# Split right operands of a three-term FFN down product made during gate and up and kept in DRAM, with output pairs visited in turn

## The chip, the cores and the metric

The kernel runs on one NeuronCore of one Trainium2 chip. The metric is device time in microseconds of that core, from launch to end. Before the change the median of three runs is 2494.79 us (2493.0 to 2496.13).

## What is computed

A two-layer encoder trunk on 1024 positions of width 1024, all in f32. Each layer is a mixer, a cross-attention into 256 memory rows and a SwiGLU feed-forward block, each behind an RMSNorm and added onto x. The change touches the feed-forward block alone:

```python
def swiglu(h, w_gate, w_up, w_down):
    return (jax.nn.silu(h @ w_gate) * (h @ w_up)) @ w_down
# per layer: w_gate, w_up (1024, 2816), w_down (2816, 1024)
x = x + swiglu(rms_norm(x, g_ffn[layer]), w_gate[layer], w_up[layer], w_down[layer])
```

## The kernel before

**Three-term products.** An f32 operand is split into two f32r parts: a high part h, which is a cast on ScalarE, and a low part l = value - h, made on VectorE (`low`, L409). A product is three matmuls: wh*xh, wh*xl, wl*xh. Everything is kept transposed: a block row of x is 128 channels by 1024 positions.

**Seven products for eight.** The feed-forward products use a Strassen-Winograd scheme with two by two blocks (`seven`). A left operand (`Unit`) is n stacked pairs of weight rows by 256 columns; from it seven parts are made with four additions, each part 128 x n*128, on the engine named `adds`. A right operand (`Pair`) is two 128 x 1024 tiles, cut into four 128 x 512 blocks; from it seven operands of 512 columns are made with four GpSimd subtractions (L307), seven casts (L318) and seven low parts (L409). Each of the seven tasks of a unit runs 3n matmuls of 512 columns into one PSUM bank. Gate and up have n = 4 (width 1024 is four pairs): 84 matmuls a unit, 22 units a layer. Down has 11 pairs of FF rows and four column pairs of the output (mp = 0 to 3).

**After a task.** `collected` gathers gate's and up's results: ScalarE copies out of PSUM (L1756, L1762, L1764) and VectorE additions (L1754). For three of the four quarters a bank is added onto again one task after it was read. `gated` applies the norm and silu with a VectorE product (L1804), a ScalarE activation (L1805) and a GpSimd product (L1806). `upped` multiplies gate and up (L1813) and stores each finished 128 x 1024 tile to the DRAM tensor `pd` (L1818), 512 KB, two for each pair of units. `onto_x` adds down's banks onto x (L1785), eight additions a unit.

**Down.** The 11 pairs are taken in four groups, DOWN = (3, 3, 3, 2 pairs). In each group the pairs' tiles are loaded from `pd` (L1856), their operands are made (GpSimd, ScalarE, VectorE as above), and all four column pairs are run with them; the units' additions are on GpSimd too (L232).

**Memory and order.** Split operands live in one arena of f32r with 35 slots of 1024 columns (`R`; a pair of h and l of 512 columns takes one slot), f32 tiles in another with 16 (`F`). During gate and up 28 slots hold the four pairs of the normed x. `run` goes through the tasks, fetches weights ahead (at most `raws` heavy ones, `f_reserve` free) and makes operands ahead as long as they are within `la` columns of the running task and `reserve` columns stay free. A scheduler then orders each engine's queue; every DMA named here is issued by SyncE (SP), whose queue runs in order, and each of its DMAs waits for the one eight before it. Down_start raises `la` from 4096 to 16384 and loads x back from `xs`. `defer` runs a step some tasks later.

## Time and profile before

| | us |
|---|---|
| median of three runs | 2494.79 |
| profiled execution, its own time | 2492.48 |
| its span, first to last instruction | 2490.7 |
| TensorE busy | 2369.1 (95%) |
| VectorE busy | 1722.8 (69%) |
| ScalarE busy | 1026.5 (41%) |
| GpSimd busy | 853.0 (34%) |
| mean granted TensorE clock | 0.973 |

Busy time of TensorE is no measure of its pace, since matmuls are pipelined and their ends are modelled: a stretch in which it is 90% busy can hold 70% of the matmuls that fit. The number of matmuls in a stretch tells the pace. Gate and up of layer 0 run from about 700 to 1100 us and down from there to about 1370; gate and up of layer 1 from about 1785 to 2225 us and down from there to the end. The view by stage gives for each engine its busy time and, in brackets, its instructions, then the granted clock as a share, the mean busy share of the 16 DMA engines, and what they moved.

### The profile page before, as it was taken

The numbers are of one execution on the slowest core, as the hardware profiler recorded it, in microseconds if no ns is written. First come the engines' busy times: TensorE is split into PE (matmuls) and PEld (weight loads), VectorE is DVE, ScalarE is ACT, GpSimd is POOL, SyncE is SP. The second block draws the span as 40 slices with busy tenths as digits, with TensorE's granted clock in tenths as the row PEclk, the third lists the DMA queues.
The fourth block names the chain that finished last, engine by engine and source line by source line (L and its number), as shares of the span: only waits on it lengthen the run. The fifth ranks groups of instructions, "written<-read, shape, count | busy, mean of one in ns | idle before, by whom it ended". The sixth has DMA issues, their size and how long they took to land. (4 is left out here: it accounts for less than half of the span.)

```text
span 2490.7 us, 30370 instructions
## 1 busy us (share of the span) xinstructions
PE 2369.1 (95%) x11246; PEld 1978.2 (79%) x11246; DVE 1722.8 (69%) x2449; ACT 1026.5 (41%) x1886; POOL 853.0 (34%) x849
## 2 busy tenths in 40 slices
PE   7999999999899999998899999999799999989998
PEld 7998889888678888876677888888588887767776
DVE  5456367855686676689989643545876767589887
ACT  5355366645543333343335221244533333344332
POOL 6551233243531112136654300132721111146551
PEclk9999999999889999999999999999799999999999
DMA  7345345421231312243222121110321231243322
GB/s 233 124 144 172 94 119 141 132 76 35 102 102 51 102 60 85 93 139 110 93 89 81 60 59 35 59 43 18 118 85 68 93 102 51 74 164 102 102 87 74
DMA packets 175836, 234.83 MB, mean 94 GB/s; under 512 B 7200, under 2 KB 145528, under 8 KB 175688
## 3 DMA queue, kind: packets, MB, share of 16 engines
q1 hardware_dynamic: 171856, 220.10, 28.1%
q0 software_dynamic: 3648, 12.75, 1.4%
q8 instruction: 88, 1.44, 0.2%
q14 instruction: 60, 0.49, 0.1%
q10 hardware_dynamic: 184, 0.05, 0.0%
HBM read 176.11 MB, written 56.75 MB: 93 GB/s over the span
## 5 line engine op out<-in xcount | busy, mean ns | idle before, releaser
L397 PE MATMUL psum_t<-arena_r 128*128 128x512 f32 (+4 forms) x10304 | 2293.3, 381 | 99.1 <-DVE arena_r L409 43.4
L397 PEld LDWEIGHTS psum_t<-arena_r 128*128 128x128 f32 (+1 forms) x10304 | 1867.5, 191 | 473.9 <-DVE arena_r L409 67.1
L409 DVE TENSOR_TENSOR arena_r<-arena_f,arena_r 128x512 fp32r<-128x512 f32 (+4 forms) x839 | 739.0, 904 | 303.5 <-ACT arena_r L241 153.6
L241 ACT CAST arena_r<-arena_f 128x512 fp32r<-128x512 f32 (+2 forms) x532 | 288.8, 563 | 565.1 <-PE psum_t L397 402.3
L1806 POOL TENSOR_TENSOR arena_f<-arena_f 128x512 f32<-128x512 f32 x88 | 135.1, 1538 | 656.3 <-ACT arena_f L1805 656.1
L307 POOL TENSOR_TENSOR arena_f<-arena_f 128x512 f32<-128x512 f32 x120 | 184.1, 1550 | 120.4 <-DMA arena_f<-pd 58.2
L232 POOL TENSOR_TENSOR arena_f<-arena_f 128x384 f32<-128x384 f32 (+1 forms) x128 | 148.2, 1166 | 103.6 <-DVE arena_r L409 51.7
L1785 DVE TENSOR_TENSOR arena_f<-psum_t,arena_f 128x512 f32<-128x512 f32 x256 | 167.7, 680 | 15.7 <-PE psum_t L397 15.0
L318 ACT CAST arena_r<-arena_f 128x512 fp32r<-128x512 f32 x210 | 123.6, 617 | 124.9 <-POOL arena_f L307 62.4
L232 DVE TENSOR_TENSOR arena_f<-arena_f 128x512 f32<-128x512 f32 x176 | 136.0, 778 | 55.6 <-DMA arena_f<-w_up 34.2
L1754 DVE TENSOR_TENSOR arena_f<-psum_t,arena_f 128x512 f32<-128x512 f32 x176 | 119.9, 685 | 33.9 <-PE psum_t L397 28.3
L527 ACT CAST arena_r<-arena_f 128x1024 fp32r<-128x1024 f32 (+1 forms) x57 | 59.0, 1042 | 109.9 <-PE psum_t L397 99.5
L409 DVE TENSOR_TENSOR arena_r<-psum_t,arena_r 128x512 fp32r<-128x512 f32 (+3 forms) x124 | 84.7, 703 | 24.9 <-ACT arena_r L1596 8.7
L1805 ACT ACTIVATE arena_f<-arena_f 128x512 f32<-128x512 f32 x88 | 55.6, 632 | 99.7 <-DVE arena_f L1804 99.2
L633 POOL TENSOR_TENSOR arena_f<-arena_f 128x1024 f32<-128x1024 f32 x21 | 60.3, 2870 | 87.0 <-ACT arena_f L632 79.7
L1259 POOL TENSOR_SCALAR arena_f<-arena_f,small 128x640 f32<-128x640 f32 (+6 forms) x64 | 49.4, 780 | 108.6 <-DVE small L1258 104.6
L1813 DVE TENSOR_TENSOR arena_f<-arena_f 128x512 f32<-128x512 f32 x88 | 73.9, 841 | 3.3
L1804 DVE TENSOR_TENSOR arena_f<-arena_f 128x512 f32<-128x512 f32 x88 | 70.7, 804 | 0.8
L420 POOL TENSOR_TENSOR small<-small,mhalf 128x4 f32<-128x4 f32 (+1 forms) x64 | 64.3, 1005 | 5.2
L1705 POOL TENSOR_TENSOR arena_f<-arena_f 128x512 f32<-128x512 f32 x28 | 43.7, 1571 | 50.7 <-ACT arena_f L1704 50.2
L1948 POOL TENSOR_TENSOR arena_f<-arena_f 128x1024 f32<-128x1024 f32 x4 | 9.6, 2392 | 140.9 <-DVE arena_f L1900 136.1
L1254 ACT ACTIVATE arena_f<-psum_t,small 128x640 f32<-128x640 f32 (+6 forms) x64 | 47.5, 744 | 23.0 <-DVE small L1252 20.1
(177 smaller groups left out, 1390.9 us busy)
## 6 DMA issues: line engine op xcount, KB each, us to landing
arena_f<-w_gate SPq DMA_DIRECT2D x22, 1024.0 KB
arena_f<-w_up SPq DMA_DIRECT2D x22, 1024.0 KB
pd<-arena_f SPq DMA_DIRECT2D x44, 512.0 KB
arena_f<-pd SPq DMA_DIRECT2D x44, 512.0 KB
arena_f<-w_down SPq DMA_DIRECT2D x24, 768.0 KB
arena_f<-xs SPq DMA_DIRECT2D x32, 512.0 KB
arena_r<-qk SPq DMA_DIRECT2D x48, 256.0 KB
xs<-arena_f SPq DMA_DIRECT2D x24, 512.0 KB
```

The costliest lines, as they stand in the source:

```text
L232: getattr(T.nc, self.adds).tensor_tensor(out=out, in0=a, in1=b, op=what)
L241: T.nc.scalar.copy(out=hv, in_=src)
L307: getattr(T.nc, self.adds).tensor_tensor(out=out, in0=a, in1=b, op=ALU.subtract)
L318: T.nc.scalar.copy(out=h.ap, in_=src)
L397: self.nc.tensor.matmul(out=out, lhsT=lhsT, rhs=rhs, start=start, stop=stop, skip_group_check=again)
L409: getattr(self.nc, eng).tensor_tensor(out=out, in0=src, in1=high, op=ALU.subtract)
L420: self.nc.gpsimd.tensor_tensor(out=out, in0=in_, in1=self.mhalf[:, 0:in_.shape[-1]], op=ALU.pow)
L1754: nc.vector.tensor_tensor(out=o, in0=bank[q].ap, in1=o if other is None else other, op=ALU.add)
L1785: nc.vector.tensor_tensor(out=o, in0=bank[q].ap, in1=o, op=ALU.add)
L1804: nc.vector.tensor_tensor(out=q, in0=q, in1=r, op=ALU.mult)
L1806: nc.gpsimd.tensor_tensor(out=q, in0=q, in1=r, op=ALU.mult)
L1813: nc.vector.tensor_tensor(out=c[j].ap[:, o], in0=c[j].ap[:, o], in1=s.ap[:, o], op=ALU.mult)
```

## The change

The right operands of down are made once, while gate and up run, and kept split. When a pair of FF tiles is finished, `store` makes its seven operands in seven steps, one step a task: the same four GpSimd subtractions (L1860), a ScalarE cast (L1864) and a VectorE low part for each. Both parts of an operand lie in one slot of the arena and go as one 512 KB store to a DRAM tensor `pq` (L1868) one task later. In down an operand is a `Stored`: two loads of 256 KB straight into the f32r arena (L339), nothing else. The units' additions in down are on VectorE (the default of `adds`).

The order in down is no longer four groups by four column pairs but a list of 14 visits (mp, first pair, last pair): each visit runs one column pair over two to four FF pairs, and the window of pairs moves on. All 44 combinations are there once. The pairs from 9 on take slots from the other end of the arena, in layer 0 from there only. The last four visits close one column pair each; the squares for the next norm are taken there, while the norm's scaled chunks of the first two are made when the last two visits open (`chunk_done` is cut in `chunk_h` and `chunk_sq`). In gate and up `la` falls from 4096 to 2048 and `reserve` rises from 0 to 3072; in down `la` is 4096.

```diff
@@
-DOWN = ((0, 1, 2), (3, 4, 5), (6, 7, 8), (9, 10))
+VISITS = ((1, 0, 1), (2, 0, 1), (3, 0, 2), (0, 0, 3), (1, 2, 4), (2, 2, 5), (3, 3, 6), (0, 4, 7), (1, 5, 8), (2, 6, 8),
+          (3, 7, 10), (0, 8, 10), (1, 9, 10), (2, 9, 10))
@@ class Stored:
+    def make(self, T, must):
+        pair = T.room_for(512, self.home, must)
+        if pair is None:
+            return False
+        self.h, self.l = pair
+        for part, t in enumerate(pair):
+            T.nc.sync.dma_start(out=t.f, in_=self.src[part].bitcast(F32))
+        return True
@@ in upped:
-
-                    def keep():
-                        nc.sync.dma_start(out=self.pd[layer, (f + j) * P:(f + j + 1) * P, :], in_=c[j].ap)
-                        c[j].free()
-                    self.defer(keep)
+                if (j, half) == (0, 1):
+                    store(f // 2, c)
             return fn
 
+        def store(pr, c):
+
+            b11, b12 = c[0].ap[:, 0:512], c[0].ap[:, 512:1024]
+            b21, b22 = c[1].ap[:, 0:512], c[1].ap[:, 512:1024]
+            t1, t2 = self.F.get(512, "ba"), self.F.get(512, "ba")
+
+            def sub(out, a, b):
+                nc.gpsimd.tensor_tensor(out=out, in0=a, in1=b, op=ALU.subtract)
+
+            def part(i, src):
+                t = self.R.get(1024, "ab")
+                nc.scalar.copy(out=t.ap[:, 0:512], in_=src)
+                self.low(t.ap[:, 512:1024], src, t.f[:, 0:512])
+
+                def keep():
+                    nc.sync.dma_start(out=self.pq[layer, pr, i].rearrange("s p c -> p s c").bitcast(F32),
+                                      in_=t.f.rearrange("p (s c) -> p s c", s=2))
+                    t.free()
+                self.defer(keep)
...
+            for n in range(7):
+                self.defer(lambda n=n: step(n), n + 1)
+
         def start():
-            self.reserve, self.la, self.raws = 0, 4096, 2
+            self.reserve, self.la, self.raws = 3072, 2048, 2
@@ in down_start:
-            self.la, self.f_reserve = 16384, 0
+            self.reserve, self.la, self.f_reserve = 0, 4096, 0
...
+        for n, (mp, lo, hi) in enumerate(VISITS):
+            left = len(VISITS) - n
+            u = Unit(wd, lo * 256, hi - lo + 1, mp * 256, "b", "b" if finish and left <= 4 else "ba")
+            if left == 2 and finish:
+                self.add(open_now)
+            if left == 1:
+                self.add(down_end)
+            self.seven(u, ps[lo:hi + 1], self.onto_x(2 * mp, quarter_of(mp, left <= 2) if left <= 4 else None))
```

Two places in the built programs. **SyncE's queue from gate and up into down, layer 0.** Before: a few stores of `pd`, then loads of `pd` and blocks of `w_down` in turn, 512 KB and 768 KB each:

```order
L222 DMA arena_f<-w_gate 128x8x256
L1818 DMA pd<-arena_f 128x1024
L222 DMA arena_f<-w_up 128x8x256
L1818 DMA pd<-arena_f 128x1024
L222 DMA arena_f<-w_down 128x6x256
L1856 DMA arena_f<-pd 128x1024 x2
L222 DMA arena_f<-w_down 128x6x256
L1883 DMA arena_f<-xs 128x1024
L1818 DMA pd<-arena_f 128x1024
L1856 DMA arena_f<-pd 128x1024
L1883 DMA arena_f<-xs 128x1024
L1818 DMA pd<-arena_f 128x1024
```

Now, from the last block of `w_up` on:

```order
L223 DMA arena_f<-w_up 128x8x256
L1868 DMA pq<-arena_r 128x2x512
L339 DMA arena_r<-pq 128x512 x5
L1966 DMA arena_f<-xs 128x1024
L339 DMA arena_r<-pq 128x512 x5
L223 DMA arena_f<-w_down 128x4x256 x2
L339 DMA arena_r<-pq 128x512 x3
L1868 DMA pq<-arena_r 128x2x512
```

and on, still on SyncE's queue, in the first two visits:

```order
L339 DMA arena_r<-pq 128x512 x21
L1868 DMA pq<-arena_r 128x2x512
L223 DMA arena_f<-w_down 128x6x256
L339 DMA arena_r<-pq 128x512 x2
L1868 DMA pq<-arena_r 128x2x512
L339 DMA arena_r<-pq 128x512
L223 DMA arena_f<-w_down 128x6x256
L339 DMA arena_r<-pq 128x512 x2
L1868 DMA pq<-arena_r 128x2x512 x4
L223 DMA arena_f<-w_down 128x8x256
L339 DMA arena_r<-pq 128x512 x24
```

The row of 24 begins with the seventh operand of pair 0. Behind the last block of `w_up` the queue now holds 39 loads of stored operands, eight stores and five blocks of `w_down` ahead of that row, where there were single tiles before.

**GpSimd's queue.** Before, in down of layer 0, subtractions of right operands (L307) and additions of the units (L232) follow each other:

```order
L307 TENSOR_TENSOR arena_f<-arena_f 128x512 x2
L232 TENSOR_TENSOR arena_f<-arena_f 128x3x128
L307 TENSOR_TENSOR arena_f<-arena_f 128x512 x2
L232 TENSOR_TENSOR arena_f<-arena_f 128x3x128
L232 TENSOR_TENSOR arena_f<-arena_f 128x384
L307 TENSOR_TENSOR arena_f<-arena_f 128x512
L232 TENSOR_TENSOR arena_f<-arena_f 128x384
L232 TENSOR_TENSOR arena_f<-arena_f 128x3x128 x6
```

Now, the end of gate and up of layer 0 and what follows: the gate products (L1839) and the subtractions of `store` (L1860), four by four, then at once the sums for the next norm (L665):

```order
L1839 TENSOR_TENSOR arena_f<-arena_f 128x512 x4
L1860 TENSOR_TENSOR arena_f<-arena_f 128x512 x4
L1839 TENSOR_TENSOR arena_f<-arena_f 128x512 x3
L1860 TENSOR_TENSOR arena_f<-arena_f 128x512 x4
L665 TENSOR_TENSOR arena_f<-arena_f 128x1024 x7
```

The subtractions moved from down into gate and up, and the units' additions left this queue.

## Rows read from the trace of the kernel before

**Rows 1.** The page, its first line

```profile
span 2490.7 us, 30370 instructions
```

**Rows 2.** By stretch: engines' busy time (instructions), clock, DMA share, GB/s

```profile
core 0: us, PE busy (x) PEld busy (x) DVE busy (x) ACT busy (x) POOL busy (x), PEclk, DMA share, GB/s
...
250.00:300.00 50.00, 50.00 (x273) 43.17 (x272) 20.04 (x23) 15.75 (x22) 14.13 (x17) 1.00 0.48 117
...
750.00:800.00 50.00, 50.00 (x222) 41.40 (x221) 33.62 (x48) 19.06 (x33) 8.15 (x6) 1.00 0.12 43
...
2250.00:2300.00 50.00, 49.93 (x221) 40.99 (x220) 47.51 (x64) 23.06 (x45) 31.16 (x24) 1.00 0.38 125
```

**Rows 3.** By stage: gate and up, down, and the end of down

```profile
730.00:1095.00 365.00, 364.38 (x1608) 301.39 (x1607) 252.62 (x362) 132.56 (x230) 59.96 (x41) 1.00 0.26 86
1100.00:1350.00 250.00, 225.33 (x935) 177.65 (x934) 227.97 (x314) 100.24 (x196) 144.58 (x107) 0.97 0.31 103
1810.00:2200.00 390.00, 381.98 (x1675) 313.29 (x1674) 270.61 (x377) 139.35 (x243) 67.62 (x44) 1.00 0.26 85
2200.00:2450.00 250.00, 220.22 (x897) 172.88 (x896) 225.95 (x306) 96.83 (x196) 139.93 (x109) 0.94 0.30 99
1350.00:1400.00 50.00, 47.06 (x208) 37.32 (x208) 32.44 (x29) 16.28 (x19) 19.52 (x10) 1.00 0.23 68
```

**Rows 4.** Waits, 1100 to 1310 us: us in total, times, longest

```profile
ACT arena_r L241 <- DMA arena_f<-w_down: 36.5, 9, 7.4
POOL arena_f L307 <- DMA arena_f<-pd: 29.5, 11, 6.1
...
PEld psum_t L397 <- DVE arena_r L409: 16.4, 14, 3.5
...
PE psum_t L397 <- DVE arena_f L1785: 12.9, 8, 2.9
```

**Rows 5.** Waits, 2220 to 2490 us

```profile
PEld psum_t L397 <- DVE arena_r L409: 19.1, 12, 4.0
...
PE psum_t L397 <- DVE arena_f L1785: 12.8, 10, 2.9
```

**Rows 6.** Groups by line, 1100 to 1310 us: count, busy us, mean ns, idle before

```profile
L409 DVE TENSOR_TENSOR arena_r<-arena_f,arena_r 128x512 fp32r<-128x512 f32 x72 | 70.8, 1015 | 6.9 <-ACT arena_r L318 6.1 <-issue 0.8
...
L307 POOL TENSOR_TENSOR arena_f<-arena_f 128x512 f32<-128x512 f32 x44 | 67.6, 1552 | 46.8 <-DMA arena_f<-pd 29.5 <-DVE arena_r L409 17.3
L232 POOL TENSOR_TENSOR arena_f<-arena_f 128x384 f32<-128x384 f32 (+1 forms) x48 | 57.8, 1214 | 30.3 <-DMA arena_f<-w_down 21.0 <-DVE arena_r L409 8.5
...
L318 ACT CAST arena_r<-arena_f 128x512 fp32r<-128x512 f32 x74 | 43.1, 619 | 53.9 <-PE psum_t L397 20.7 <-POOL arena_f L307 16.9 <-DMA arena_f<-pd 16.2
```

**Rows 7.** The same for 730 to 1095 us, shapes kept apart

```profile
L409 DVE TENSOR_TENSOR arena_r<-arena_f,arena_r 128x512 fp32r<-128x512 f32 x133 | 100.2, 758 | 69.1 <-ACT arena_r L241 59.3 <-PE psum_t L397 9.5
...
L232 DVE TENSOR_TENSOR arena_f<-arena_f 128x512 f32<-128x512 f32 x70 | 52.7, 757 | 18.2 <-DMA arena_f<-w_up 10.5 <-DMA arena_f<-w_gate 6.2 <-DMA pd<-arena_f 0.7
```

**Rows 8.** In order of time, VectorE and GpSimd: start, us, instruction

```profile
802.36 0.69 DVE L1754 TENSOR_TENSOR arena_f<-psum_t,arena_f 128x512 f32<-128x512 f32 x1 [2.39 <-PE psum_t L397]
802.97 0.68 DVE L409 TENSOR_TENSOR arena_r<-arena_f,arena_r 128x512 fp32r<-128x512 f32 x1
...
810.36 1.46 DVE L232 TENSOR_TENSOR arena_f<-arena_f 128x512 f32<-128x512 f32 x1
...
809.98 1.29 POOL L1806 TENSOR_TENSOR arena_f<-arena_f 128x512 f32<-128x512 f32 x1 [3.70 <-ACT arena_f L1805]
```

**Rows 9.** By stretch, two with the DMA engines nearly or fully busy

```profile
2225.00:2235.00 10.00, 5.00 (x10) 2.77 (x11) 7.06 (x9) 4.56 (x8) 4.75 (x4) 0.67 1.00 341
182.00:202.00 20.00, 18.75 (x157) 18.36 (x157) 15.80 (x34) 15.12 (x34) 5.02 (x9) 1.00 0.91 303
```

**Rows 10.** Waits of TensorE's weight loads, 2060 to 2200 us

```profile
PEld psum_t L397 <- ACT arena_f L1764: 7.1, 5, 1.4
```

**Rows 11.** The page's list of DMA issues

```profile
pd<-arena_f SPq DMA_DIRECT2D x44, 512.0 KB
```

More of the change, by code (lines that the diff above doesn't have):

```diff
@@ L1847, in down_end, with open_now @@
+        def open_now():
+            opening()
+            for k in waiting:
+                finish(k)
         def down_end():
             self.la, self.reserve = 3072, 0
[L1850 to L1878 removed]
@@ L2048, in build @@
         self.cross(0, pairs[0])
[L2049 removed]
+        self.ffn(0, pairs[0], lambda m: self.chunk_h("mix", 1, m), self.open_h)
         self.odd()
```

123 lines of the change are left out of this document (74 added, 49 removed).

## The prediction

> **What bounds the kernel now.** I read the table by stage first, then the waits of the two down products, then what their costliest groups cost beside each other. TensorE takes 222 matmuls of 512 columns in 50 us when nothing holds it [rows 2], 0.2252 us each. Gate and up of layer 0 run at that pace: 1608 in 365 us, which is 0.227 us each [rows 3]. The two down products do not. From 1100 to 1350 us there are 935 where 1110 fit, so 175 x 0.2252 = 39.4 us are lost; from 2200 to 2450 us 897, so 48.0 us are lost [rows 3]. Together that is 87.4 us, and it is all that an edit of the down product can win: the matmuls themselves stay (44 pair-and-column products a layer, 7 x 3 matmuls each, 924, as before; the built programs hold equally many). Gate and up of layer 1 lose (1732 - 1675) x 0.2252 = 12.8 us of their own [rows 3].
>
> What TensorE waits for in the down products is not one thing. It waits for the low parts (L409, VectorE) and for VectorE's additions onto x (L1785), at each some 12 to 19 us, by matmul and weight load [rows 4, 5]. VectorE is busy 228 of 250 us there [rows 3], since L409 of 512 columns takes 1015 ns where it takes 758 in gate and up [rows 6, 7]. Before that stand GpSimd's subtractions, 67.6 and 57.8 us [rows 6], and before these the loads of pd and w_down, 29.5 and 36.5 us [rows 4]. It is a chain of load, subtraction, cast and low part, with every link nearly full.
>
> **What makes L409 long.** On VectorE the ops at 802.36 and 802.97 us start 0.61 us apart and take 0.69 and 0.68 us each; the one at 810.36 us takes 1.46 us while GpSimd's product (L1806) runs from 809.98 to 811.27 us [rows 8]. So a VectorE op with both inputs in SBUF costs 0.61 us alone, and up to 0.78 us more beside GpSimd.
>
> **What leaves the down product.** Per layer 77 casts, 77 low parts and 44 GpSimd subtractions for the right operands go. At 1.015 us [rows 6] the low parts are 78 us of VectorE in a stage of some 250. The 16 x 4 left-operand additions move from GpSimd to VectorE as 14 x 4; at no more than 0.76 us [rows 7] that is 43 us, less for narrow visits. Additions onto x fall from 128 to 112, which I leave out of the sum. VectorE's 228 us become 228 - 78 + 43 = 193 us of the 250 at most, and fewer as GpSimd has nothing left there and no op is stretched any more. The visits of two pairs are the tight ones, with 8 additions, 4 sums and 7 low parts for 9.4 us of matmuls. I price those at nothing: from 2250 to 2300 us VectorE is 47.5 of 50 us busy while TensorE takes 221 matmuls [rows 2], so a full VectorE alone does not stop it.
>
> **What comes instead in the down product: bytes.** Each right operand is now two loads of 256 KB, 154 loads or 40.4 MB a layer in place of 11.5 MB. With w_down (11.5 MB) that is 52 MB, 152 us at 341 GB/s, the rate at which the DMA engines were fully busy [rows 9]. On average that fits into 208 us. The start does not. 28 of the arena's 35 slots of 1024 columns hold gate's operands, so the first stored load can go only when the last up unit gives up its first slots. From there to the seventh operand of pair 0, in the order in which SyncE issues them, layer 0 has 40 loads (10.5 MB), 7 stores that are still due for pairs 9 and 10 (3.7 MB), one load of x and five w_down blocks (4.2 MB): 18.4 MB, 54 us at 341 GB/s. TensorE has 176 matmuls until it needs that operand (68 of the last up unit, 108 of the visits), 39.6 us. It is short by 14 us. Layer 1, counted in the same way up to an operand in the third visit, has 22.8 MB or 67 us against 249 matmuls or 56 us, short by 11 us. Behind these points TensorE has been delayed by more than any later load is short, and each later load has a visit's time. I add 4 us a layer for landing times and for the lower clock after the wait (the stretch from 2225 to 2235 us shows 0.67 [rows 9]). So the down products lose 18 + 15 = 33 us where they lost 87.4: **54 us won**. At 303 GB/s, the mean of the next best long stretch [rows 9], the two are short by 21 and 19 us, and 39 us are won; if loads never bind, about 80.
>
> **What moves into gate and up.** Per pair of units (168 matmuls, 37.8 us) come 7 casts, 7 low parts, 4 GpSimd subtractions and 7 stores of 512 KB instead of 2 [rows 11]. In the 365 us read above lie 9.6 pairs: 67 low parts x 0.61 = 41 us, and 38 subtractions that can each hold up VectorE by 0.78 us = 30 us. VectorE was idle for 365 - 252.6 = 112 us there [rows 3], so 41 us remain and TensorE stays the bound. ScalarE has 132.6 us of 365 [rows 3] and takes 67 casts x 0.62 us [rows 6] = 42 more. DMA share doubles from 0.26 [rows 3]. On SyncE's queue the 77 stores stand between the weight loads, each waiting for its low part; a weight load that is held behind one has about one unit, 18.9 us, before its first part is due. The look-ahead of left parts is halved (4096 to 2048 columns, some four tasks of 2.7 us).
>
> What this costs is not in the trace. The nearest row is a ScalarE copy out of PSUM (L1764) that made TensorE wait 5 times, 1.4 us at most, 7.1 us in all [rows 10]: such a copy has one task, 2.7 us, before its bank is written again, and ScalarE's queue now holds casts that wait for a store to have landed. A gain is possible too, since the shuffled order could remove these 7 us. I take +5 us a layer, with bounds of -7 in layer 1 alone and +25 for both layers (about one wait of 1.1 us a pair). End of layer 0: four chunks of the next norm are made when the last two visits open, and two each behind them, beside 84 matmuls; 1350 to 1400 us loses (222 - 208) x 0.2252 = 3 us now [rows 3], and I leave it so. Everything before the first gate unit is ordered as before.
>
> **Sum.** The profiled execution took 2492.48 us with a span of 2490.7 us [rows 1], 1.8 us lying around it. 2492.5 - 54 + 10 = 2448.5 us; the median of the three runs is 2.3 us above that execution, so **2451 us**.
>
> **Rivals.**
> A. The loads run slower than 341 GB/s. For it: they are 256 KB, half of the pd loads, and the stretch from 250 to 300 us moved 117 GB/s at a busy share of 0.48, which is 244 GB/s if all were busy [rows 2]. Against it: 341 GB/s at full share [rows 9] came out of several transfers in flight, and the built program lets eight be out. At 244 GB/s the transitions are short by 36 and 37 us, 81 with the 8 us, and 6 us are won against 10 paid: 2499 us, no change.
> The Trainium skill has a rule that would push further: "SBUF — State Buffer", section "The DMA setup-cost knee", sees a 256 KiB transfer at 224 GB/s, since some 2 us of each do not scale with its bytes, and advises the largest single transfers. By that figure the change would lose about 10 us and end at 2514 us; no run here has yet shown 256 KB loads back to back, and the row at 341 GB/s is of 512 and 768 KB loads.
> B. **Slower:** ScalarE becomes the bound of gate and up. The place is the cast of a stored operand that waits until the store before it in the same slot has landed, with the PSUM copy of the running unit behind it; TensorE then stops at that bank. The decisive point is a stop of 54 / 22 = 2.5 us in each of the 22 pairs; at 3.5 us it is 77 us, and the time is 2492.5 - 54 + 77 + 2.3 = 2518 us. For it: copies already stop TensorE in layer 1 [rows 10], and only seven slots are shared by parts and stores. Against it: the slots are used 21 times in 37.8 us, some 12 us a use, while a store needs cast, low part and landing, perhaps 6 to 8.
>
> **Chances.** Forecast 0.74, its own range 2415 to 2481 (all loads hidden and no cost in gate and up, 2492.5 - 80 + 2.3 = 2415; 303 GB/s and +25 us, 2492.5 - 39 + 25 + 2.3 = 2481). A 0.13, from 2481 at 303 GB/s to 2499 and beyond; about 0.02 of it is the page's rule. B 0.13, from 2490 up. Range for 8 in 10: 2418 to 2492. A measurement here tells 0.2% from no change, 5 us: faster 0.82 (forecast and the milder half of A), same 0.06, slower 0.12.
>
> **What will show it.** Right, if TensorE takes over 215 matmuls in every 50 us of down except the first 50 to 60 us of each, if its only long waits there are for loads from pq, if GpSimd is idle there, if L409's successor costs about 0.69 us there, and if gate and up stay above 218 per 50 us with VectorE near 44 of 50 us. Wrong, if waits for pq go on into the later visits (A), if gate and up fall below 215 per 50 us with TensorE waiting for ScalarE's copies (B), or if VectorE is over 48 of 50 us busy there.

## The result and the profile after

The changed kernel takes 2463.28 us (median of 4, 2460.71 to 2464.76) against 2494.55 us of the kernel before on the same chip (median of 4): a ratio of 0.9874, 95% interval 0.9856 to 0.9891. It is 31.3 us faster; some 44 were forecast, and the time lies in the range. The profiled execution has a span of 2463.0 us, 27.7 less than that of [rows 1].

The page of the kernel after, first its busy times, then three of its groups (busy us, mean ns, then the idle time before them):

```profile
span 2463.0 us, 30890 instructions
PE 2355.2 (96%) x11246; PEld 1973.7 (80%) x11246; DVE 1729.0 (70%) x2501; ACT 1023.0 (42%) x1858; POOL 747.0 (30%) x721
...
L1818 DVE TENSOR_TENSOR arena_f<-psum_t,arena_f 128x512 f32<-128x512 f32 x224 | 148.1, 684 | 59.3 <-PE psum_t L421 58.6
L1860 POOL TENSOR_TENSOR arena_f<-arena_f 128x512 f32<-128x512 f32 x88 | 144.0, 1657 | 73.8 <-DVE arena_f L1846 72.1
L1787 DVE TENSOR_TENSOR arena_f<-psum_t,arena_f 128x512 f32<-128x512 f32 x176 | 119.7, 683 | 36.8 <-PE psum_t L421 23.7
```

In the new code L1860 is the subtraction, L1864 the cast and L1868 the store of a stored operand, L339 its load, L1818 the addition onto x (L1785 before), L1787 the sum out of PSUM in gate and up (L1754 before), L433 the low part (L409 before). The same five stages as in [rows 3], of the kernel after (stretch, then busy time of PE, PEld, DVE, ACT and POOL with the number of instructions, clock, DMA share, GB/s):

```profile
730.00:1095.00 365.00, 359.25 (x1576) 294.72 (x1574) 316.98 (x417) 164.40 (x290) 136.13 (x77) 1.00 0.44 153
1100.00:1350.00 250.00, 235.00 (x1013) 190.47 (x1011) 177.51 (x297) 73.44 (x130) 19.98 (x10) 0.98 0.70 237
1810.00:2200.00 390.00, 381.11 (x1659) 309.47 (x1657) 333.40 (x434) 170.15 (x303) 142.62 (x81) 1.00 0.42 146
2200.00:2450.00 250.00, 237.89 (x1042) 194.91 (x1043) 173.82 (x299) 65.50 (x125) 10.55 (x7) 0.97 0.72 245
1350.00:1400.00 50.00, 47.61 (x201) 38.70 (x202) 30.87 (x22) 13.39 (x16) 17.83 (x11) 0.93 0.17 54
```

Down went from 935 and 897 matmuls in 250 us to 1013 and 1042 (the last with some smaller ones of the kernel's end, which comes sooner), with VectorE down from 228 and 226 busy us to 178 and 174. Gate and up went the other way: 1608 to 1576 and 1675 to 1659, with VectorE up by 64 and 63 us. Inside down the loss has its main place at the start (finer stretches, same columns; at the other end, from 1300 to 1350 us, there are 207 matmuls where 222 fit):

```profile
1100.00:1125.00 25.00, 23.64 (x101) 18.21 (x100) 16.48 (x35) 10.80 (x24) 4.54 (x2) 1.00 0.84 288
1125.00:1150.00 25.00, 15.40 (x63) 12.10 (x63) 21.20 (x38) 6.70 (x13) 5.55 (x4) 0.87 1.06 388
1150.00:1200.00 50.00, 48.06 (x204) 39.24 (x204) 36.01 (x62) 13.19 (x24) 0.00 (x0) 0.96 0.87 307
1200.00:1250.00 50.00, 50.00 (x223) 41.38 (x222) 34.41 (x56) 11.44 (x20) 0.00 (x0) 1.00 0.72 237
1250.00:1300.00 50.00, 50.00 (x222) 41.42 (x221) 28.78 (x51) 8.86 (x16) 0.00 (x0) 1.00 0.75 244
```

From 1125 to 1150 us the DMA engines are full at 388 GB/s and TensorE does 63 matmuls where 111 fit, at a granted clock of 0.87 on the mean: TensorE stands still for 9.1 us until 1148.25 us, and from 1145 to 1150 us the clock is 0.50, the lower of its two levels (1.2 and 2.4 GHz). From 1200 to 1300 us it misses nothing. The waits of 1100 to 1310 us that answer to [rows 4] (us in total, times, longest):

```profile
DVE arena_f L233 <- DMA arena_f<-w_down: 29.4, 12, 6.3
...
PEld psum_t L421 <- ACT arena_r L242: 14.8, 7, 9.6
...
PE psum_t L421 <- DVE arena_f L233: 9.1, 1, 9.1
```

TensorE's waits for low parts and for additions onto x are gone from their head; what is left is weight parts (L242) of w_down blocks and the sums for them (L233). VectorE, which makes these sums, waits 29.4 us for such blocks to land; SyncE issues them between the loads of pq.

Every trace here holds 11246 TensorE matmuls, so two kernels can be laid beside each other by the number of matmuls done. That shows where time is gained without the stages' own shifts. The table is worked out from the starts of the matmuls in each trace, in us:

```
matmuls      what lies there                        before   after   difference
   0- 3800   all before gate and up of layer 0       699.8   700.4     +0.6
3800- 5490   gate and up, layer 0                    384.4   388.6     +4.2
5490- 5900   last gate and up unit, start of down    118.1   116.3     -1.7
5900- 6490   the rest of down, layer 0               146.9   134.1    -12.8
6490- 6620   end of layer 0, odd mixer begins         31.6    35.9     +4.4
6620- 8390   odd mixer, cross-attention              379.1   376.2     -3.0
8390- 8500   start of gate, layer 1                   52.0    57.3     +5.4
8500-10150   gate and up, layer 1                    384.7   386.5     +1.9
10150-10560  last gate and up unit, start of down    117.6   113.9     -3.7
10560-11246  the rest of down, layer 1               171.2   148.3    -22.9
```

### The profile page after: what moved, and what is told of

It reads as the page before. It is cut to its first block, busy times and chain, and to the rows that moved or that the text cites. A ratio compares the mean times of both kernels' runs of the same rounds, so it can differ in the third digit from the quotient of the medians.

```text
span 2463.0 us, 30890 instructions
## 1 busy us (share of the span) xinstructions
PE 2355.2 (96%) x11246; PEld 1973.7 (80%) x11246; DVE 1729.0 (70%) x2501; ACT 1023.0 (42%) x1858; POOL 747.0 (30%) x721
## 3 DMA queue, kind: packets, MB, share of 16 engines
q8 instruction: 88, 1.44, 0.2%
## 5 line engine op out<-in xcount | busy, mean ns | idle before, releaser
L433 DVE TENSOR_TENSOR arena_r<-arena_f,arena_r 128x512 fp32r<-128x512 f32 (+4 forms) x811 | 702.8, 886 | 183.1 <-ACT arena_r L242 49.5
L242 ACT CAST arena_r<-arena_f 128x512 fp32r<-128x512 f32 (+2 forms) x504 | 284.0, 584 | 464.1 <-PE psum_t L421 259.0
L1839 POOL TENSOR_TENSOR arena_f<-arena_f 128x512 f32<-128x512 f32 x88 | 164.4, 1875 | 497.5 <-ACT arena_f L1838 497.5
L233 DVE TENSOR_TENSOR arena_f<-arena_f 128x512 f32<-128x512 f32 (+2 forms) x288 | 211.0, 736 | 85.5 <-DMA arena_f<-w_down 52.6
L1818 DVE TENSOR_TENSOR arena_f<-psum_t,arena_f 128x512 f32<-128x512 f32 x224 | 148.1, 684 | 59.3 <-PE psum_t L421 58.6
L1864 ACT CAST arena_r<-arena_f 128x512 fp32r<-128x512 f32 x154 | 95.5, 621 | 197.6 <-DVE arena_f L1846 70.4
L1860 POOL TENSOR_TENSOR arena_f<-arena_f 128x512 f32<-128x512 f32 x88 | 144.0, 1657 | 73.8 <-DVE arena_f L1846 72.1
L1787 DVE TENSOR_TENSOR arena_f<-psum_t,arena_f 128x512 f32<-128x512 f32 x176 | 119.7, 683 | 36.8 <-PE psum_t L421 23.7
L665 POOL TENSOR_TENSOR arena_f<-arena_f 128x1024 f32<-128x1024 f32 x21 | 60.9, 2898 | 273.9 <-ACT arena_f L661 176.0
L551 ACT CAST arena_r<-arena_f 128x1024 fp32r<-128x1024 f32 (+1 forms) x57 | 59.0, 1042 | 114.4 <-PE psum_t L421 97.7
L433 DVE TENSOR_TENSOR arena_r<-psum_t,arena_r 128x512 fp32r<-128x512 f32 (+3 forms) x124 | 84.6, 703 | 23.3 <-ACT arena_r L1653 7.3
L1846 DVE TENSOR_TENSOR arena_f<-arena_f 128x512 f32<-128x512 f32 x88 | 77.1, 876 | 4.9 <-POOL arena_f L1839 1.2
L1837 DVE TENSOR_TENSOR arena_f<-arena_f 128x512 f32<-128x512 f32 x88 | 63.3, 720 | 0.1
L1738 POOL TENSOR_TENSOR arena_f<-arena_f 128x512 f32<-128x512 f32 x28 | 43.0, 1551 | 50.6 <-ACT arena_f L1737 50.2
L296 POOL TENSOR_TENSOR arena_f<-arena_f 128x512 f32<-128x512 f32 x32 | 50.8, 1605 | 11.5 <-PE psum_t L421 7.4
```

Of the source, the lines that this page charges most:

```text
L233: getattr(T.nc, self.adds).tensor_tensor(out=out, in0=a, in1=b, op=what)
L242: T.nc.scalar.copy(out=hv, in_=src)
L433: getattr(self.nc, eng).tensor_tensor(out=out, in0=src, in1=high, op=ALU.subtract)
L1787: nc.vector.tensor_tensor(out=o, in0=bank[q].ap, in1=o if other is None else other, op=ALU.add)
L1818: nc.vector.tensor_tensor(out=o, in0=bank[q].ap, in1=o, op=ALU.add)
L1837: nc.vector.tensor_tensor(out=q, in0=q, in1=r, op=ALU.mult)
```

## The experiments

All stand on the kernel after unless said otherwise, and all ratios are to the kernel before run on the same chip (2492.3 to 2492.7 us). The kernel after itself ran where the kernel before took 2494.55 us, so a difference of 2 us between an experiment and it says nothing. Any edit lets the scheduler put the engines' instructions into another order, also in stages that the edit does not touch, and each row below is one profiled execution (the four runs of a kernel lie 1.6 to 6.1 us apart). How far a stage moves that is not edited can be seen in e2, e3, e8 and e9, which touch down only: gate and up of layer 0 by up to 1.1 us, of layer 1 by -6.5 to +5.5, the start of gate by 3.5, the starts (e3, e8) by 1.4. Less than that says nothing of a cause.

Not all of this is another order. The +5.5 us of e3 arise in the first 75 matmuls of that stage: a stretch at a lower clock (0.62 and 0.70 from 1805 to 1815 us) lies in it, which in the kernel after lies largely ahead of it (0.66 from 1805 to 1810 us, then 1.00). Behind them VectorE, ScalarE, GpSimd and SyncE run in the same order as there, and with the start of gate, which is 3.5 us shorter, +2.0 is left. In e2 the order does differ, and 5 of its 6.5 us lie between the 8650th and the 8950th matmul. There e1, e10, e12 and e13 gain 4 to 6 us as well, so that much of their gain in gate and up of layer 1 is not shown to come from their edits.

The stages of all kernels, as differences to the kernel after, in us (the two starts are 5490-5900 and 10150-10560, the two gate/up 3800-5490 and 8500-10150 of the table above; the rest of down is within 0.3 us of the kernel after in all but the last row):

```
                     gate/up 0  start 0  end 0  gate start 1  gate/up 1  start 1
e1  no making          -4.6     -23.4    -3.6     -1.2        -12.5      -20.6
e2  quarter loads      -0.7      -9.7    -1.6     -0.3         -6.5       -3.6
e3  adds on GpSimd     -0.3      +0.4    -2.5     -3.5         +5.5       +1.4
e8  one load           +0.6      +1.1    -0.3     +0.1         -0.3       -0.3
e9  last pair late     +1.1      -8.8    -1.5     -1.0         +1.7       -8.4
e10 no store           -2.1      -9.5    -1.9     -1.5         -6.9       -8.9
e12 subs on VectorE    -4.4      -1.3    -1.6     -1.5         -8.3       -2.3
e13 look-ahead 4096    -1.2      -2.8    -1.4     -3.0         -6.7       -6.4
e14 e9 + e12 + e13     -3.4      -9.4    -1.6     +0.2        -11.4      -11.8
e15 and L1839          -2.7      -9.5    -1.3     -4.7         -7.0      -11.6
e17 and GpSimd queue   -2.0      -6.1    -1.4     -4.1         -4.2      -11.4
e5  before, adds only  (against before: down -1.5, -1.7, -1.3 and -7.4)
```

### What the making costs (e1, e10)

```diff
@@ e1: upped()
-                    store(f // 2, c)
+                    c[0].free()
+                    c[1].free()
@@ e10: part()
                 def keep():
-                    nc.sync.dma_start(out=self.pq[layer, pr, i].rearrange("s p c -> p s c").bitcast(F32),
-                                      in_=t.f.rearrange("p (s c) -> p s c", s=2))
                     t.free()
@@ both: Stored.make(), with wg = self.kv[layer] and n counted through the operands
-            T.nc.sync.dma_start(out=t.f, in_=self.src[part].bitcast(F32))
+            n = self.n + part
+            T.nc.sync.dma_start(out=t.f, in_=self.wg[n % 4, :, n // 4 % 2 * 512:n // 4 % 2 * 512 + 512].bitcast(F32))
```

> The kernel after, without the making of the stored operands: no casts, low parts, subtractions or stores of them in gate and up; each load of down reads other stored bytes of the same size, so that the down product loads and multiplies as before. It leaves out the right operands of the down product. Theory M (the making costs little by itself, the two starts of down are short of bytes): gate and up win back the 4 us of layer 0 and the 2 us of layer 1 that the matmul counts show against the kernel before; each start of down has the 7 last stores (3.7 MB, 11 us at 341 GB/s) less to move and loses 6 to 9 us in place of 17 to 19. Together 2463 - 6 - 22 = about 2435 us. Rival S (the starts are late because loads and weight blocks are issued late and in the wrong order, not for bytes): the starts still lose 15 us or more each, about 2455 us. Rival V (VectorE beside GpSimd in gate and up costs far more than 6 us and hides in the start of down): below 2425 us.

2399.84 us (ratio 0.9626, 0.961 to 0.9642), below what any theory but V had. Theory M falls: the making costs 63 us in all, not some 28. At most 17 of them are in gate and up; 44 are in the two starts of down, in which TensorE never stands still here. The same 50 us as above by stretch, in e1, with as many loads of 256 KB (of eight blocks of another tensor in turn):

```profile
1100.00:1125.00 25.00, 25.00 (x112) 20.70 (x111) 17.31 (x33) 5.02 (x13) 1.28 (x1) 1.00 1.06 381
1125.00:1150.00 25.00, 25.00 (x112) 20.69 (x111) 20.64 (x38) 8.14 (x16) 0.00 (x0) 1.00 0.83 276
```

The loads as such are therefore hidden: the DMA engines are full there too, at 381 GB/s, and TensorE does not wait. In e1 the first stored operand is asked for when TensorE has begun 5505 matmuls, in the kernel after at 5519; by the 22nd load they are 5568 and 5608. In e10, which makes the operands and leaves out their stores, they are 5519 and 5605: it is not the stores that make the loads late.

> The kernel after, with the stored operands made as there but not stored: their slots come free when the low part is done; the loads read other stored bytes of the same size. It leaves out the right operands of the down product. Theory M (in gate and up it is the work on VectorE and GpSimd that costs, not the stores): gate and up keep their loss (some 4 us in layer 0, some 11 in layer 1 beside the run without making), and the starts lose up to 9 us less each for 3.7 MB of stores fewer: 2445 to 2455 us. Rival B (casts that wait for a store's landing hold ScalarE and with it the copies out of PSUM): gate and up come down to the run without making as well, below 2435 us.

2432.65 us (0.9761, 0.9747 to 0.9776): B's number. Leaving out the stores alone gives back 9.5 and 8.9 us of the starts and 2.1 and 6.9 of gate and up. M had the starts right. In gate and up the 2.1 us of layer 0 are more than a stage moves that is not edited, the 6.9 of layer 1 are not; so rival B of the prediction costs at most 9 us in 22 pairs, 0.4 us a pair. How such a wait acts is to be seen at the last gate unit of layer 0, in the kernel after in order of time (start, us, engine, instruction; in brackets the idle time before it and what ended it):

```profile
1085.49 5.76 DVE L433 TENSOR_TENSOR arena_r<-arena_f,arena_r 128x512 fp32r<-128x512 f32 x4
1085.64 6.75 POOL L1860 TENSOR_TENSOR arena_f<-arena_f 128x512 f32<-128x512 f32 x4 [1.23 <-DVE arena_f L1846]
...
1092.46 0.62 ACT L1864 CAST arena_r<-arena_f 128x512 fp32r<-128x512 f32 x1 [2.80 <-POOL arena_f L1860]
1093.12 0.69 DVE L433 TENSOR_TENSOR arena_r<-arena_f,arena_r 128x512 fp32r<-128x512 f32 x1 [1.86 <-ACT arena_r L1864]
1094.14 0.62 ACT L1864 CAST arena_r<-arena_f 128x512 fp32r<-128x512 f32 x1 [1.06 <-DMA pq<-arena_r]
1094.29 0.42 SPq L223 DMA_DIRECT2D arena_f<-w_up  x1
1094.66 0.58 ACT L1797 COPY arena_f<-psum_t 128x512 f32<-128x512 f32 x1
1094.79 0.69 DVE L433 TENSOR_TENSOR arena_r<-arena_f,arena_r 128x512 fp32r<-128x512 f32 x1 [0.98 <-ACT arena_r L1864]
1095.40 0.68 DVE L1787 TENSOR_TENSOR arena_f<-psum_t,arena_f 128x512 f32<-128x512 f32 x1
...
1096.14 1.22 PE L421 MATMUL psum_t<-arena_r 128*128 128x512 f32 x2 [4.27 <-DVE arena_f L1787]
```

Read it from below. TensorE waits 4.27 us for a sum out of PSUM (L1787). That sum stands in VectorE's queue behind two low parts of stored operands. These wait for their casts, the first cast for a subtraction on GpSimd, the second for a store to have landed; the copy out of PSUM (L1797) stands behind it on ScalarE. And four low parts before them took 1.44 us each beside four GpSimd subtractions of 1.69. It is the place and the sort of wait that rival B named, though it stops TensorE by VectorE's sum rather than by ScalarE's copy.

### Bytes, sizes and the tail of the making (e2, e8, e9)

```diff
@@ e2: Stored.make()
-            T.nc.sync.dma_start(out=t.f, in_=self.src[part].bitcast(F32))
+            T.nc.sync.dma_start(out=t.f[:, 0:128], in_=self.src[part][:, 0:128].bitcast(F32))
@@ e8: Stored.make()
-        pair = T.room_for(512, self.home, must)
...
-        for part, t in enumerate(pair):
-            T.nc.sync.dma_start(out=t.f, in_=self.src[part].bitcast(F32))
+        t = T.R.alloc(1024, self.home)
...
+        T.nc.sync.dma_start(out=t.f.rearrange("p (s c) -> p s c", s=2),
+                            in_=self.src.rearrange("s p c -> p s c").bitcast(F32))
@@ e9: store()
+            late = (0, 1) if pr < NF // 2 - 1 else (14, 3)
             for n in range(7):
-                self.defer(lambda n=n: step(n), n + 1)
+                self.defer(lambda n=n: step(n), n * late[1] + 1 + late[0])
```

> The kernel after, with each load of a stored operand cut to the first 128 of its 512 columns (64 KB in place of 256 KB), as many loads at the same places; the rest of the tile keeps what was there. It leaves out three quarters of the right operands of the down product. Theory M (bytes bind the starts of down): to the seventh operand of pair 0 there are 18.4 - 7.9 = 10.5 MB, 31 us at 341 GB/s against 39.6 us of matmuls, so each start loses 0 to 5 us instead of 17 to 19; 2463 - 28 = about 2435 us, gate and up unchanged. Rival S (late issue, slots, landing time): both starts lose 15 us or more, 2455 to 2463 us.

2442.92 us (0.9806, 0.9791 to 0.982), between the two theories. With a quarter of the bytes of these loads the starts still lose 13.7 and 17.1 us beside those of e1 (92.9 and 93.2 us), though the DMA engines are now busy at 0.55 and 0.79 from 1100 to 1125 and to 1150 us. So the loads' bytes are a part and not the whole: 9.7 us in layer 0, 3.6 in layer 1. The 6.5 us in gate and up of layer 1, where nothing is loaded from pq, go with another order of VectorE's, ScalarE's and SyncE's queues there.

> The kernel after, with the two parts of each stored operand in neighbouring slots and one load of 512 KB in place of two of 256 KB; as many bytes. Theory M (the starts are bound by bytes at a rate that does not depend on the size of a load): as the kernel after, within 5 us, 2458 to 2468 us, and the two starts move 335 to 345 GB/s as they do now. Rival A (loads of 256 KB are slow, larger ones are not): the starts lose 8 to 10 us less each, 2445 us or below, at a higher rate. The Trainium skill's rule in 'SBUF - State Buffer', section 'The DMA setup-cost knee', is on the side of A: by its figures a transfer of 256 KiB moves 224 GB/s and one of 1 MiB 341.

2464.32 us (0.9892, 0.9877 to 0.9906): no change. Rival A falls, and the rule of the Trainium skill ("SBUF — State Buffer", "The DMA setup-cost knee"), 224 GB/s for 256 KiB, does not hold in this kernel. The fullest stretch of its first start, with loads of 512 KB (columns as above):

```profile
1125.00:1150.00 25.00, 20.05 (x74) 15.33 (x73) 23.25 (x44) 7.72 (x15) 5.64 (x4) 0.86 1.06 389
```

389 GB/s against 388 with loads of 256 KB. With many transfers in flight their size makes no difference here.

> The kernel after, with the seven steps that make the operands of the last pair (pair 10) moved from tasks 1 to 7 behind its unit to every third task from the 15th on, into the down product; that pair is first needed in the eleventh of 14 visits. Nothing is left out. Theory M (the start of down loses most of its time to the tail of the making: 7 casts, 7 low parts, 4 subtractions and 3.7 MB of stores that stand between the first loads): each start loses 8 to 12 us less, about 2443 us. Rival S (it is the loads alone, which cannot go before the last unit of up gives up its slots): no change within 4 us, 2459 to 2467 us. Rival L (the steps then disturb the later visits, which run at full rate now): the visits of 1150 to 1250 us fall below 210 matmuls per 50 us and nothing is won.

2442.27 us (0.9797, 0.9779 to 0.9814). Each start loses 8.8 and 8.4 us less, and the later visits keep their pace (the rest of down takes 134.1 and 148.3 us as before): theory M for the tail. So of the 44 us of the starts, some 17 come from the seven steps and stores of the last pair that stand among the first loads. e10 takes away 18 without moving the steps, so it is likely their stores; the two were not tried together.

### Which engine (e3, e5, e12)

```diff
@@ e3: ffn(), the units of down (e5: the same place of the kernel before, "gpsimd" to "vector")
-            u = Unit(wd, lo * 256, hi - lo + 1, mp * 256, "b", "b" if finish and left <= 4 else "ba")
+            u = Unit(wd, lo * 256, hi - lo + 1, mp * 256, "b", "b" if finish and left <= 4 else "ba", "gpsimd")
@@ e12: store()
             def sub(out, a, b):
-                nc.gpsimd.tensor_tensor(out=out, in0=a, in1=b, op=ALU.subtract)
+                nc.vector.tensor_tensor(out=out, in0=a, in1=b, op=ALU.subtract)
```

> The kernel after, with the additions of the left operands of the down product back on GpSimd, as in the kernel before. Theory O (the down product won because 77 low parts, 77 casts and 44 subtractions a layer left it): GpSimd has 56 additions a layer, some 1.5 us each, and VectorE has room for being stretched by them; the later visits stay above 215 matmuls per 50 us and the time is 2463 to 2472 us. Rival G (it won because GpSimd stands still beside VectorE): the visits behind the start fall to 185 to 200 matmuls per 50 us, as in the kernel before, and the time is 2485 us or more.

> The kernel before, with one part of the change alone: the additions of the left operands of the down product on VectorE instead of GpSimd. Nothing is left out. Theory O (the down product of the kernel before is bound by the making of its operands, low parts above all, whoever does the additions): 64 additions of some 0.6 us come to VectorE's 228 of 250 us and about as much stretching goes; down wins less than 15 us a layer, 2465 to 2500 us. Rival G (GpSimd's additions beside VectorE were the loss): down loses less than 15 us a layer, 2445 us or below.

e3 takes 2465.04 us (0.9897, 0.9882 to 0.9912), e5 2480.53 (0.9951, 0.9937 to 0.9966): theory O in both. In e3 the low parts of down are stretched again, and it costs nothing, since VectorE has room. Of e3, one stretch of the visits, and then two groups of 1150 to 1310 us:

```profile
1200.00:1250.00 50.00, 50.00 (x223) 41.40 (x222) 29.18 (x42) 11.64 (x19) 17.08 (x14) 1.00 0.73 245
```

```profile
L433 DVE TENSOR_TENSOR arena_r<-arena_f,arena_r 128x512 fp32r<-128x512 f32 x42 | 35.8, 865 | 11.6 <-ACT arena_r L242 10.0 <-PE psum_t L421 1.2
L233 POOL TENSOR_TENSOR arena_f<-arena_f 128x512 f32<-128x512 f32 x24 | 32.9, 1373 | 64.5 <-DMA arena_f<-w_down 38.9 <-DVE arena_r L433 24.7
```

In the kernel after the same low parts take 685 ns. The additions' move to VectorE is worth 12 us in the kernel before, where VectorE is full, and behind the change 2 us by the medians and 6 by the ratios at the most. What won the down product, then, is that the making of its right operands left it. The trace of the kernel before says the same: by shape, 9.6 of the 10.8 us that its matmuls wait for low parts from 1100 to 1310 us are for parts of 512 columns, which are the right operands' there. The order of the visits came with the change and was not run alone.

> The kernel after, with the four subtractions a pair that make the stored operands on VectorE instead of GpSimd (1.66 us each there). Nothing is left out. Theory P (such a subtraction on GpSimd holds VectorE up by about as long as it would take there itself, 0.6 to 0.7 us, and its result is late by a further microsecond): VectorE's busy time in gate and up stays within 3 us per 100, the casts come sooner, and gate and up with the start of down win 4 to 12 us, 2451 to 2459 us. Rival W (VectorE's own queue is the limit, each operation on it counts): VectorE is busier and the time is 2468 us or more.

2445.77 us (0.9818, 0.9803 to 0.9832), more than P expected. From 730 to 1095 us VectorE has 40 subtractions of its own and is yet less busy, 306.3 us against 317.0 (kernel after above). The groups of low parts there, first of the kernel after, then of e12 with its subtractions, and e12's stretch:

```profile
L433 DVE TENSOR_TENSOR arena_r<-arena_f,arena_r 128x512 fp32r<-128x512 f32 x198 | 172.1, 892 | 16.7 <-ACT arena_r L242 8.3 <-ACT arena_r L1864 6.6 <-PE psum_t L421 0.4
```

```profile
L433 DVE TENSOR_TENSOR arena_r<-arena_f,arena_r 128x512 fp32r<-128x512 f32 x198 | 138.2, 724 | 12.8 <-ACT arena_r L1864 7.2 <-ACT arena_r L242 4.2 <-PE psum_t L421 1.1
L1860 DVE TENSOR_TENSOR arena_f<-arena_f 128x512 f32<-128x512 f32 x40 | 26.6, 686 | 0.4
```

```profile
730.00:1095.00 365.00, 360.60 (x1589) 297.51 (x1587) 306.30 (x463) 167.03 (x293) 69.53 (x39) 1.00 0.46 157
```

Forty subtractions on GpSimd, 1.66 us each, made 198 low parts longer by 34 us; on VectorE they take 27. The stage table has the gain in gate and up, where the prediction had charged it: 4.4 us in layer 0, which is beyond what an unedited stage moves, and 8.3 in layer 1, which is little beyond it.

### The look-ahead, and what the edits give together (e13, e14, e15, e17)

```diff
@@ e13: start()
-            self.reserve, self.la, self.raws = 3072, 2048, 2
+            self.reserve, self.la, self.raws = 3072, 4096, 2
@@ e14: e9, e12 and e13 together; e15: also gated()
-            nc.gpsimd.tensor_tensor(out=q, in0=q, in1=r, op=ALU.mult)
+            nc.vector.tensor_tensor(out=q, in0=q, in1=r, op=ALU.mult)
@@ e17: e15, and keep()
-                    nc.sync.dma_start(out=self.pq[layer, pr, i].rearrange("s p c -> p s c").bitcast(F32),
+                    nc.gpsimd.dma_start(out=self.pq[layer, pr, i].rearrange("s p c -> p s c").bitcast(F32),
```

> The kernel after, with the look-ahead of prepared operands in gate and up at 4096 columns, as in the kernel before, instead of 2048. Nothing is left out. Theory H (the halved look-ahead costs the start of gate in layer 1, 5 us, and some of the waits for weight parts in gate and up of layer 1): 2453 to 2460 us, with 1750 to 1800 us back from 96 to some 115 matmuls. Rival N (the order at that start changed for another reason): within 4 us of 2463 us, or slower where more parts take the slots of the stored operands.

2441.29 us (0.9798, 0.9783 to 0.9812), 22 us below the kernel after, twice what H had, and not where H had it. The start of gate in layer 1 gets 3 us back, no more than e3 gets there without an edit; 9.2 us come from the two starts, and 6.7 from gate and up of layer 1, about what e2 gets there without an edit. That the look-ahead matters in the starts is the part that stands; the prediction had named its halving and given it no price. Why it matters there was not followed up.

> The kernel after with three edits that were each run alone: the making of the last pair spread into the down product (2442 us alone), the subtractions of the making on VectorE (2446 us alone), the look-ahead at 4096 columns (2441 us alone). Nothing is left out. Theory T (three separate places: the first removes 10 us at each start of down, the two others mostly waits in gate and up, which they partly share): 2463 - 20 - 14 to 22 = 2420 to 2430 us. Rival U (one chain, which each of them shortens enough): 2438 us or more. By the run without any making (2400 us) no version that still makes the operands is expected below 2405 us.

2424.01 us (0.9725, 0.9709 to 0.9741): theory T, and the best version here, 39 us below the kernel after and 68 below the kernel before. The starts have little more than e9's gain, gate and up 14.8 us where e12 alone had 12.7 and e13 7.9.

> The three edits together, and the multiplication behind the gate's activation on VectorE too instead of GpSimd, where it took 1.88 us; GpSimd then has nothing left in gate and up. Nothing is left out. Theory P (beside a running GpSimd operation a VectorE operation with both inputs in SBUF takes up to 0.7 us longer, so that VectorE is no busier when it does the work itself): VectorE's busy share in gate and up stays within 3 us per 100, no low part is over 0.75 us there, and the time is 0 to 8 us below the kernel with three edits. Rival W (VectorE's queue becomes the bound): VectorE over 46 of 50 us, and a longer time than with three edits.

2426.02 us (0.9733, 0.9718 to 0.9747), the same as e14. P holds for VectorE: with GpSimd idle from 730 to 1095 us it is 307.8 us busy, though it now has 79 operations that GpSimd had, and the low part is at its own pace (the stretch, then the group):

```profile
730.00:1095.00 365.00, 361.52 (x1585) 298.04 (x1584) 307.82 (x499) 167.66 (x292) 0.00 (x0) 1.00 0.45 157
```

```profile
L433 DVE TENSOR_TENSOR arena_r<-arena_f,arena_r 128x512 fp32r<-128x512 f32 x197 | 131.5, 687 | 13.1 <-ACT arena_r L242 7.1 <-ACT arena_r L1864 3.5 <-PE psum_t L421 2.1
```

It gives no time; P's range for the time is missed by 2 us.

> The kernel with four edits (2426 us), and the stores of the operands issued by GpSimd, which is idle there, instead of SyncE, where they stand between the loads of w_gate, w_up and w_down. Nothing is left out. Theory Q (SyncE's order holds weight loads behind stores that wait for their low part, and stores behind weight loads that wait for room; ScalarE's casts of stored operands then wait 3.7 us for a landing and TensorE 2 to 5 us, twice in the tenth pair of each layer): the waits at the start of the last gate unit (2.5 and 1.7 us in layer 0, 1.7 and 4.4 in layer 1) go, and one wait for w_down at the start of down: 2412 to 2420 us. Rival N (the transfers are what takes long, not their place in a queue): 2422 to 2430 us. Rival D (issuing on GpSimd takes it longer, since it shares a path to SBUF with VectorE, and stores land later): over 2430 us. The Trainium skill's page 'SBUF - State Buffer' tells of such a trap for transfers issued from GpSimd beside VectorE; that would be D.

2433.26 us (0.9763, 0.9747 to 0.978), 7 us slower than e15. Theory Q falls; the number is D's. A store takes GpSimd 0.73 us to issue where SyncE took 0.36 in the kernel after, and ScalarE's casts of weight parts wait 21.0 us for landings where they waited 9.2 in e15 (groups of 730 to 1000 us, of e17):

```profile
L242 ACT CAST arena_r<-arena_f 128x512 fp32r<-128x512 f32 x98 | 59.4, 620 | 84.9 <-PE psum_t L421 57.4 <-DMA pq<-arena_r 21.0 <-issue 3.8
...
L1868 POOL DMA_DIRECT2D pq<-arena_r x49 | 35.7, 728 | 241.1 <-DVE arena_r L433 241.1
```

That VectorE holds up the issuing, as D has it, is not shown by this: an issue takes 0.73 us in the median and 0.83 at the most, beside a VectorE that is busy for 229 of the 270 us. Why the kernel is slower stays open. The Trainium skill, "DMA: Bandwidth & Descriptors", section "Issuing engines are not separate DMA queues", says that another issuing engine saves only its sequencer's time; the run agrees that nothing is won; that it loses is not in that rule.

## Why the prediction was right, step by step

**What bound the kernel before: right.** The low parts, casts and subtractions of the right operands. VectorE in down came to 177.5 and 173.8 busy us of 250 (at most 193 was written), L433 of 512 columns to 685 ns (0.69), GpSimd to nothing from 1150 to 1300 us. e3 and e5 show that the additions, which the change moves too, were not the main of it. One row was misread on the way: of "GpSimd's subtractions, 67.6 and 57.8 us" the 57.8 are the units' additions [rows 6]; no term of the sum rests on it.

**The rest of down: right.** "Behind these points TensorE has been delayed by more than any later load is short": 590 matmuls in 134.1 us are 0.2273 each, within 1% of the full pace, and the 134.1 us are the same within 0.3 in every kernel that has the stored operands.

**The starts: the right place, 11 us too little, and a sum that came near for partly wrong reasons.** 33 us were written. Beside e1, whose starts lose nothing, the kernel after loses 116.3 - 92.9 = 23.4 and 113.9 - 93.2 = 20.7, together 44. The step that failed is the equation of the loss with the bytes. The rate was not 341 but 388 GB/s, so the 18.4 MB take 47 us and not 54, and TensorE should have been 8 us short and not 14. About that much, 9 to 10 us in layer 0, goes with a quarter of the loads (e2), without stores (e10), or with the last pair made and stored later (e9), one at a time; the prediction had counted just these stores. The other 13 us stay when three quarters of the loaded bytes go (e2), and go when the making goes (e1).

The trace of the kernel after tells where most of the 23.4 us lie. TensorE stands still for 17.2 us: 9.1 for the sum of a w_down block that landed late (L233 among the waits above), 3.3 for two more weight parts, 4.3 at the last gate unit, from the chain shown at e10, and 0.5 for an addition onto x. The seventh operand of pair 0, of which the prediction counted it short, is not among these waits. And for part of the time it runs at the lower clock, which costs some 4 us, an estimate from the granted clock while TensorE is busy; the prediction's 4 us a layer were to cover this and the landing. In layer 1 it stands still for 13.8 us, 5.6 of them for a weight part and 4.8 at the last gate unit. So the prediction lacked the wait at the last gate unit, and the clock alone takes the 4 us that it had put down for clock and landing. Which part of the making (casts, slots, subtractions) makes the loads later by 14 to 40 matmuls is left open, since e1 removes all of them at once; the stores alone do not (e10).

**Gate and up: +6 us against +10, but two things in one number.** The making costs at most 4.6 + 12.5 = 17 us (after beside e1), and perhaps 11, since e2, which keeps it, has 6.5 of the 12.5 too. Against that stands a gain that the prediction had only as a bound: without the making, gate and up of layer 1 take 374.0 us where the kernel before took 384.7, so 10.7 of the 12.8 us that were lost there are gone, more than the 7 us of ScalarE's copies [rows 10]. Whether the new order did that, or that e1 stores nothing there where the kernel before stores its finished tiles, was not separated. VectorE's 44 of 50 us were right (317 of 365 is 43.4); "TensorE stays the bound" was not, since it waits for VectorE with VectorE at 87%: what counts is where an operation stands in VectorE's queue, and the four low parts of 1.44 us beside GpSimd stand in one row. The price of a subtraction beside VectorE, which the prediction read in [rows 8] and entered as busy time alone, is what e12 gives back.

**The end of layer 0, "I leave it so": wrong by 4.4 us.** Part of it is the clock, 0.93 from 1350 to 1400 us where it was 1.00 [rows 3], which is 3.5 us of these 50; it is 0.50 from 1352.4 to 1355 us, behind the wait shown here. In the last visit two low parts of the odd mixer's weights, 1024 columns wide, stand ahead of the sums that free TensorE's banks, beside a square sum on GpSimd (of the kernel after, VectorE, GpSimd and TensorE apart):

```profile
1347.85 4.49 DVE L433 TENSOR_TENSOR arena_r<-arena_f,arena_r 128x1024 fp32r<-128x1024 f32 x2
1352.26 1.27 DVE L1818 TENSOR_TENSOR arena_f<-psum_t,arena_f 128x512 f32<-128x512 f32 x2
```

```profile
1347.80 3.45 POOL L665 TENSOR_TENSOR arena_f<-arena_f 128x1024 f32<-128x1024 f32 x1 [7.29 <-issue]
```

```profile
1352.39 1.22 PE L421 MATMUL psum_t<-arena_r 128*128 128x512 f32 x2 [3.62 <-DVE arena_r L433]
```

No run changed this order alone. **The start of gate in layer 1** was not in the sum either and costs 5.4 us. It lies between 52.6 and 57.5 us in the kernels run here, 52.0 before, also where nothing near it is edited; its cause is open.

**The sum.** Forecast from the profiled execution: -54 + 10 = -44 us. Measured: down -41.1 (-1.7 - 12.8 - 3.7 - 22.9), gate and up +6.1, the two seams +9.8, the rest -2.4: -27.6. The down product won 13 us less than written, gate and up gave 4 back, and two seams that had been left at nothing cost 10.

**Rivals.** A falls: more bytes a load change nothing (e8), and the rate was above, not below, the one assumed. B is small: at most 0.4 us a pair hang on stores, where 2.5 us a pair would have been needed for a slower kernel. Of "What will show it", the visits from 1200 to 1300 us, GpSimd, L433 and VectorE came as said; the last 50 us of down in layer 0, with 207 matmuls, did not; "only long waits there for pq" did not: TensorE's longest wait in down, 9.6 us, was for a weight part; and gate and up fell to 208 and 195 matmuls per 50 us from 1000 to 1100 us, and to 204 to 217 in most stretches of layer 1, below the 215 that had been named as the sign of B.

## What to carry over

Work moved out of a full stage can cost more than its busy time where it lands: it matters where it stands in the queues there. Look for the copies and sums out of PSUM that come behind it, and for what the last piece of it delays at the seam. When transfers bind only at one seam, first take out of it what is not due yet: the making and the stores of the last pair were worth some 20 us here, in two lines (e9). A GpSimd operation beside a full VectorE should be priced at what it adds to VectorE's queue: moving the subtractions there made VectorE less busy (e12). And a stage that an edit does not touch can still move by several us from one kernel to the next, so a gain must be larger than that, or be seen in the whole kernel's time.

## What the runs showed of the hardware that was not expected

- Loads of 256 KB, with stores among them, ran at 388 GB/s for 25 us (share of the DMA engines 1.06), and loads of 512 KB at 389. The prediction had taken 341 from the fullest stretch of the kernel before.
- A VectorE operation with both inputs in SBUF takes 687 ns while GpSimd is idle (e15) and 892 on the mean where GpSimd is busy for 136 of 365 us (the kernel after); one that reads PSUM takes 683 and 684 either way (L1787 in gate and up, L1818 in down, of the page above). The Trainium skill, "SBUF — State Buffer", section "SBUF: two separate sides", has it that a VectorE operation with two inputs in SBUF and a GpSimd operation that reads SBUF take turns at one pair of ports for a whole instruction; the rows agree, four low parts of 1.44 us each standing beside four subtractions of 1.69 (at e10).
- A store takes 0.73 us to issue on GpSimd (e17) and 0.36 on SyncE (the kernel after).
